# Low parts of the weights by transfers that add the raw tile onto the negated rounded one, in a two-block transformer kernel

## The chip, the cores and the metric

The kernel runs on one core of a Trainium2 chip. The metric is the device time of one execution in microseconds (us), the median of several runs. Engines are named TensorE (PE in the profile, PEld for its weight loads), VectorE (DVE), ScalarE (ACT), GpSimd (POOL) and SyncE (SP); 16 DMA engines move data for all of them.

## The reference, cut to what matters

The program is a chain of dense layers on 512 tokens of width 1024, all in fp32: a mixer with pooling and a gated spatial branch, a feed-forward layer with a convolution, a gated embedding layer, then two layers of feed-forward, attention, feed-forward. Nearly all arithmetic is activations times a weight matrix that is read once:

```python
def swiglu(h, wg, wu, wd):
    return (jax.nn.silu(h @ wg) * (h @ wu)) @ wd
...
for i in range(DEPTH_2):
    x = x + 0.5 * swiglu(rmsnorm_2(x, ffn_norm1[i]), ffn1_wg[i], ffn1_wu[i], ffn1_wd[i])
    h = rmsnorm_2(x, mix_norm[i])
    ...
    x = x + 0.5 * swiglu(rmsnorm_2(x, ffn_norm2[i]), ffn2_wg[i], ffn2_wu[i], ffn2_wd[i])
```

with inner widths of 2816 in the feed-forward layers and 1024 to 5120 elsewhere.

## The kernel before, in words

**Split products.** TensorE multiplies in a rounded format (fp32r in the profile). To keep fp32 accuracy each operand is split into a rounded part h and a low part lo = raw - h, and a product is three matmuls: h·h, h·lo and lo·h. A weight tile is 128x1024 (CH = 1024 columns, 512 KB) in nearly all places; it holds 8 blocks of 128x128, so 24 matmuls use it. `Weights._load` brings a raw tile (`wr`) from memory by a transfer on SyncE's queue (L717 to L720), `_split` takes two more tiles, `wh` and `wl`, and calls `_parts` (L728): ScalarE copies raw into `wh`, which rounds it, and VectorE writes raw - `wh` into `wl`. The first weight tile is handled in four pieces of 256 columns (`first`), and some tiles of the attention stages are 512, 416 or 384 columns wide. `wr`, `wh`, `wl`, `ws` and the activations' operand tiles (`op`, `opf`, `th`, `tl`, `tt`, `bb`) all share one pool of 34 buffers.

**Plain and fast stages.** The mixer, the convolution layer, the embedding layer, the first feed-forward layer and the attentions use each weight tile as it is. The other three feed-forward layers (`fast_swiglu`) save one product in eight by Strassen's scheme: `_sums` (L733) loads 4 raw tiles, makes 3 sums and differences on VectorE (`ws`, and one raw tile that is overwritten), and splits 7 tiles in all; each is used by 24 matmuls with 256 columns. This is a block; a stage has 9 of them. `fast_order` sets the order: 8 plain tiles first (4 pairs), then blocks, with the tiles of the down projection ("down chunks") in between, 16 before the end of the last block and 6 after it.

**The order of the work.** The program is first recorded as a list of operations. `Order.arrange` (a list scheduler with its own costs, buffer counts and transfer times) then decides in which order the operations stand on each engine; each engine executes its own list in order and waits on semaphores for what it needs. `Weights.next` records the load and split of a tile four tiles ahead of its use (AHEAD = 3), and the scheduler may move them further ahead as buffers allow. All operations are emitted at L691, so every row of the profile has that line and the tiles' names tell them apart. Transfers of weights stand on SyncE's queue, five small transfers (positions, bias table, p) on GpSimd's; GpSimd otherwise does some elementwise work in the mixer and the softmax products of the attentions.

Of the kernel before, what the change touches and what calls it, by code (L numbers as in the profile page):

```python
# [10 lines left out]
F32 = mybir.dt.float32  # L11
# [3 lines left out]
AF = mybir.ActivationFunctionType  # L15
ALU = mybir.AluOpType
# [13 lines left out]
CH = 1024  # L30
# [666 lines left out]
class Weights:  # L697
# [28 lines left out]
        return h, lo  # L726

    def _parts(self, raw, h, lo):  # L728
        self.nc.scalar.copy(out=h, in_=raw)
        self.nc.vector.tensor_tensor(out=lo, in0=raw, in1=h.bitcast(F32), op=ALU.subtract)  # L730


    def _sums(self):  # L733
# [1209 lines left out]
```

## Time and profile before

| | |
|---|---|
| median of 3 runs | 2630.89 us (2630.42 to 2632.65) |
| the profiled execution | 2632.25 us, of which the span is 2630.5 us |
| TensorE busy | 2605.5 us (99%) |
| VectorE busy | 1846.0 us (70%) |
| ScalarE busy | 1072.0 us (41%) |
| GpSimd busy | 126.3 us (5%) |
| DMA queue of SyncE | 251.31 MB, 28.9% of 16 engines' span |
| software queue (GpSimd) | 0.92 MB, 0.1% |

The span is the profiled execution from its first to its last instruction. A busy share is an average over stages with different limits; matmuls are pipelined, so the mean time of one matmul is longer than the step from one to the next. The granted TensorE clock is full (0.9 or more) in all slices of the page. TensorE is never idle for long, and the chain of work that ended last runs through its matmuls.

### The profile page before, as it was taken

The page shows a single profiled execution, that of the slowest core. Times are in us where ns is not written, and L with a number is a line of the kernel's source. Part 1 is how long each engine was busy: PE and PEld are TensorE (multiplying, and loading weights), DVE is VectorE, ACT ScalarE, POOL GpSimd, SP SyncE. Part 2 cuts the span into 40 slices and gives each one's busy share as a digit, 9 for nine tenths or more (in the row PEclk, how much of TensorE's full clock was granted, in tenths as well). Part 3 has the DMA queues.
Part 4 walks back from the last instruction along what each step waited for, and adds up shares of the span by engine and source line. Part 5 has one row for each costly group of instructions (what it writes and reads, how often), then busy time and mean ns, then how long its engine had stood idle before and what let it go on. Part 6 is the DMA issues. An engine that isn't in the chain of part 4 may idle for free. (4 is left out here: it accounts for less than half of the span.)

```text
span 2630.5 us, 36927 instructions
## 1 busy us (share of the span) xinstructions
PE 2605.5 (99%) x14732; PEld 2225.9 (85%) x14732; DVE 1846.0 (70%) x3076; ACT 1072.0 (41%) x1658; POOL 126.3 (5%) x193
## 2 busy tenths in 40 slices
PE   9999999999999999999999999999999999999999
PEld 7888888888888888889788999889999866789998
DVE  7525487969957944445778777787777686787774
ACT  5333333323444323233743433533434475543342
POOL 1100000000000000001400000000000142000000
PEclk9999999999999999999999999999999999999999
DMA  5232232333322423234131323413233101213332
GB/s 200 96 113 79 98 111 72 98 119 121 116 93 81 133 82 122 88 98 132 52 112 57 111 99 105 153 33 112 89 105 136 31 17 61 88 57 113 105 104 81
DMA packets 103037, 254.60 MB, mean 97 GB/s; under 512 B 37376, under 2 KB 39296, under 8 KB 102864
## 3 DMA queue, kind: packets, MB, share of 16 engines
q1 hardware_dynamic: 102560, 251.31, 28.9%
q8 instruction: 116, 1.90, 0.3%
q0 software_dynamic: 304, 0.92, 0.1%
q14 instruction: 57, 0.47, 0.1%
HBM read 242.76 MB, written 9.44 MB: 96 GB/s over the span
## 5 line engine op out<-in xcount | busy, mean ns | idle before, releaser
L691 PE MATMUL ps<-op,wh 128*128 128x512 f32 x3840 | 1194.9, 392 | 3.4 <-ACT wh L691 2.4
L691 PEld LDWEIGHTS ps<-op,wh 128*128 128x128 f32 x3840 | 717.6, 188 | 157.4 <-issue 5.2
L691 PE MATMUL ps<-op,wl 128*128 128x512 f32 x1920 | 749.5, 390 | 0.0
L691 DVE TENSOR_TENSOR wl<-wr,wh 128x1024 fp32r<-128x1024 f32 (+3 forms) x471 | 543.6, 1162 | 126.3 <-ACT wh L691 55.5
L691 ACT CAST wh<-wr 128x1024 fp32r<-128x1024 f32 (+3 forms) x471 | 459.9, 991 | 324.5 <-DMA wr<-in_w 170.8
L691 PEld LDWEIGHTS ps<-op,wl 128*128 128x128 f32 x1920 | 360.4, 188 | 76.3 <-issue 1.2
L691 DVE TENSOR_TENSOR f<-ps,f 128x512 f32<-128x512 f32 x233 | 160.1, 689 | 251.0 <-PE ps L691 209.6
L691 PE MATMUL pt<-op,wh 128*128 128x512 f32 x1056 | 326.3, 391 | 3.4 <-ACT op L691 3.3
L691 PE MATMUL ps<-th,wl 128*128 128x256 f32 x864 | 244.5, 283 | 0.0
L691 PE MATMUL ps<-tl,wh 128*128 128x256 f32 x864 | 244.5, 283 | 0.0
L691 PE MATMUL ps<-th,wh 128*128 128x256 f32 x864 | 244.4, 283 | 0.0
L691 PE MATMUL ps<-bb,wh 128*128 128x256 f32 x1296 | 236.8, 283 | 0.0
L691 PEld LDWEIGHTS pt<-op,wh 128*128 128x128 f32 x1056 | 196.3, 188 | 45.3 <-ACT op L691 4.5
L691 PE MATMUL pt<-op,wl 128*128 128x512 f32 x528 | 205.0, 389 | 0.0
L691 PEld LDWEIGHTS ps<-bb,wh 128*128 128x128 f32 x1296 | 202.2, 192 | 0.0
L691 PE MATMUL ps<-bb,wl 128*128 128x256 f32 x648 | 183.4, 283 | 0.0
L691 ACT CAST op<-f 128x512 fp32r<-128x512 f32 x136 | 83.2, 620 | 238.7 <-DVE f L691 218.9
L691 PEld LDWEIGHTS ps<-tl,wh 128*128 128x128 f32 x864 | 165.8, 192 | 1.0
L691 PEld LDWEIGHTS ps<-th,wh 128*128 128x128 f32 x864 | 165.8, 192 | 0.9
L691 PEld LDWEIGHTS ps<-th,wl 128*128 128x128 f32 x864 | 165.8, 192 | 0.1
L691 PE MATMUL ps<-wh,op 128*128 128x256 f32 (+3 forms) x608 | 147.9, 330 | 0.3 <-ACT opf L691 0.3
L691 DVE TENSOR_TENSOR f<-f 128x512 f32<-128x512 f32 (+1 forms) x186 | 121.0, 651 | 35.3 <-ACT f L691 25.8
(211 smaller groups left out, 2829.6 us busy)
## 6 DMA issues: line engine op xcount, KB each, us to landing
wr<-in_w SPq DMA_DIRECT2D x411, 512.0 KB, 4.2
wr<-in_w SPq DMA_DIRECT2D x40, 256.0 KB, 2.8
bias<-e SPq DMA_DIRECT2D x28, 256.0 KB, 2.9
opf<-bias SPq DMA_DIRECT2D x16, 448.0 KB, 4.2
x<-in_xT SPq DMA_DIRECT2D x8, 256.0 KB, 4.5
out_y<-x SPq DMA_DIRECT2D x7, 256.0 KB, 2.0
wr<-in_w SPq DMA_DIRECT2D x4, 416.0 KB, 6.1
wr<-in_w SPq DMA_DIRECT2D x12, 128.0 KB, 4.1
```

Source lines behind the costliest of these rows:

```text
L691: getattr(getattr(self.nc, o.eng), o.name)(*[real(a) for a in o.args], **{k: real(v) for k, v in o.kw.items()})
```

## The change

For tiles of 1024 columns the subtraction on VectorE is dropped. ScalarE, which has just written the rounded tile `wh`, writes its negative into `wl` by a second activation (scale -1), and a transfer from GpSimd's queue then adds the raw tile onto `wl` (`accum_op`). Narrower tiles keep the subtraction. The transfer reads `wr` (or `ws`) and `wl` from on-chip memory and writes `wl`; `wr` cannot be reused, and `wl` cannot be multiplied with, before it has landed.

```diff
     def _parts(self, raw, h, lo):
-        self.nc.scalar.copy(out=h, in_=raw)
-        self.nc.vector.tensor_tensor(out=lo, in0=raw, in1=h.bitcast(F32), op=ALU.subtract)
+        nc = self.nc
+        nc.scalar.copy(out=h, in_=raw)
+        if raw.shape[1] == CH:
+            nc.scalar.activation(out=lo, in_=h.bitcast(F32), func=AF.Copy, scale=-1.0)
+            nc.gpsimd.dma_start(out=lo, in_=raw, accum_op=ALU.add)
+        else:
+            nc.vector.tensor_tensor(out=lo, in0=raw, in1=h.bitcast(F32), op=ALU.subtract)
```

The scheduler sees other operations with other costs, so the order on all engines is made anew. 492 transfers of the form `wl<-wr` or `wl<-ws` now stand on GpSimd.

ScalarE at the first block of the first fast stage, before (CAST is the rounding copy, `ps` are TensorE's sums that ScalarE evicts):

```order
L691 CAST wh<-ws 128x1024 x2
L691 CAST op<-f 128x512
L691 CAST wh<-wr 128x1024 x2
L691 CAST wh<-ws 128x1024
L691 CAST wh<-wr 128x1024
L691 COPY f<-ps 128x512
L691 CAST wh<-wr 128x1024
L691 ACTIVATE f<-ps 128x256
```

The same place with the change:

```order
L691 CAST wh<-ws 128x1024
L691 ACTIVATE wl<-wh 128x1024 x2
L691 CAST wh<-wr 128x1024
L691 ACTIVATE wl<-wh 128x1024 x2
L691 CAST wh<-wr 128x1024
L691 ACTIVATE wl<-wh 128x1024 x2
L691 CAST wh<-ws 128x1024
L691 ACTIVATE wl<-wh 128x1024
L691 COPY f<-ps 128x512
```

Each rounding copy is followed by a negation, often of the tile before, and the eviction of `ps` stands behind them.

GpSimd between the last softmax product of the first attention and the second attention, before (no weight work at all):

```order
L691 TENSOR_TENSOR opf<-opf,aden 128x128
L691 TENSOR_TENSOR opf<-opf,aden 128x768
L691 COPY opf<-bkrot 128x4x32 x2
L691 TENSOR_TENSOR f<-opf,tcbqr 128x128
L691 TENSOR_TENSOR f<-opf,tsbqr 128x4x16
```

GpSimd at the first block of the first fast stage with the change, each transfer with the semaphores that it waits for (DMAHW: transfers of SyncE's queue, DMASW: of GpSimd's own, the rest are engines):

```order
L691 DMA wl<-ws 128x1024 [waits DMASW6_49,DVE_49,Activation_49]
L691 DMA wl<-wr 128x1024 [waits DMAHW3_49,DMASW1_49,Activation_49]
L691 DMA wl<-wr 128x1024 [waits DMASW2_49,DVE_49,Activation_49]
L691 DMA wl<-ws 128x1024 [waits DMASW7_49,DMASW5_49,Activation_49]
L691 DMA wl<-wr 128x1024 [waits DMASW3_49,DMAHW4_49,DMASW0_49,Activation_49]
L691 DMA wl<-wr 128x1024 [waits DMAHW2_49,DMASW6_49,Activation_49]
L691 DMA wl<-ws 128x1024 [waits DMASW4_49,DVE_49,Activation_49]
```

The seven tiles of a block are seven transfers in a row, each behind ScalarE's negation.

TensorE at the start of the program, at the second weight tile, before (`mcol` matmuls are the mean of squares):

```order
L691 MATMUL ps<-op,wh 128x512 [waits Activation_49]
L691 MATMUL ps<-op,wl 128x512 [waits DVE_49]
L691 MATMUL ps<-op,wh 128x512 x2
L691 MATMUL ps<-op,wl 128x512
L691 MATMUL ps<-op,wh 128x512 x2
```

The same place with the change:

```order
L691 MATMUL ps<-op,wh 128x512 [waits Activation_49]
L691 MATMUL ps<-op,wh 128x512
L691 MATMUL pt<-mcol,f 128x1 [waits DVE_49]
L691 MATMUL pt<-mcol,f 128x1 x3
L691 MATMUL ps<-op,wh 128x512 [waits Activation_49]
L691 MATMUL ps<-op,wh 128x512
L691 MATMUL ps<-op,wh 128x512 [waits PE_49,Activation_49]
L691 MATMUL ps<-op,wh 128x512
L691 MATMUL pt<-f,ones 128x512 [waits DVE_49]
L691 MATMUL ps<-op,wl 128x512 [waits DMASW0_49]
```

TensorE now does the matmuls with rounded weights and the two norm matmuls first, and comes to its first transferred low part behind them.

## Rows read from the trace of the kernel before

**Rows 1.** Section 1 of the page: busy us (share) xinstructions:

```profile
PE 2605.5 (99%) x14732; PEld 2225.9 (85%) x14732; DVE 1846.0 (70%) x3076; ACT 1072.0 (41%) x1658; POOL 126.3 (5%) x193
```

**Rows 2.** TensorE's waits: what it waited for: total us, times, longest:

```profile
PE pt L691 <- ACT op L691: 3.3, 3, 1.1
...
PE pt L691 <- DVE opf L691: 2.7, 1, 2.7
...
PE ps L691 <- DVE op L691: 1.4, 3, 0.7
PE pt L691 <- DVE op L691: 1.2, 1, 1.2
```

**Rows 3.** Chain that ended last, in order of time: start us, us, what:

```profile
2418.40 20.15 PE ps L691 x168
2438.55 10.91 PE pt L691 x48
...
2573.70 20.15 PE ps L691 x168
2593.85 32.68 PE pt L691 x144
```

**Rows 4.** VectorE groups, 2418.4 to 2449.46: xcount | busy us, mean ns | idle:

```profile
L691 DVE TENSOR_TENSOR wl<-wr,wh 128x1024 fp32r<-128x1024 f32 x6 | 7.3, 1221 | 0.3
L691 DVE TENSOR_TENSOR wl<-ws,wh 128x1024 fp32r<-128x1024 f32 x3 | 3.7, 1223 | 1.2 <-ACT wh L691 1.2
```

**Rows 5.** DMA, 2418.4 to 2449.46: packets, MB, share; issues, us to landing:

```profile
q1 hardware_dynamic: 864, 3.15, 30.7%
...
wr<-in_w SPq DMA_DIRECT2D x6, 512.0 KB, 3.6
```

**Rows 6.** Stretches: length; busy of PE, PEld, DVE, ACT, POOL; clock; DMA share:

```profile
900.00:1000.00 100.00, 100.00 (x463) 82.72 (x462) 51.42 (x112) 24.44 (x30) 0.00 (x0) 1.00 0.31 95
2418.40:2449.46 31.06, 31.06 (x218) 29.17 (x218) 22.70 (x27) 11.82 (x15) 0.00 (x0) 1.00 0.31 103
```

**Rows 7.** VectorE on low parts, 900 to 1000 us: count, min/median/max ns:

```profile
L691 DVE TENSOR_TENSOR wl<-wr,wh x17: 1215/1218/1227, 900.3 to 994.7; 128x1024 fp32r<-128x1024 f32 x17
```

**Rows 8.** Groups by shape, whole span: xcount | busy us, mean ns:

```profile
L691 DVE TENSOR_TENSOR wl<-wr,wh 128x1024 fp32r<-128x1024 f32 x411 | 500.4, 1226 | 123.4 <-ACT wh L691 55.1 <-PE ps L691 50.9 <-PE pt L691 7.6
L691 ACT CAST wh<-wr 128x1024 fp32r<-128x1024 f32 x411 | 425.6, 1046 | 316.4 <-DMA wr<-in_w 167.9 <-PE ps L691 74.0 <-DVE wl L691 37.9
...
L691 DVE TENSOR_TENSOR wl<-ws,wh 128x1024 fp32r<-128x1024 f32 x81 | 98.9, 1221 | 11.0 <-ACT wh L691 10.4
```

**Rows 9.** GpSimd at L691: count, min/median/max ns, first and last start:

```profile
L691 POOL DMA_DIRECT2D f<-in_pT x2: 536/536/536, 680.5 to 681.7; - x2
```

**Rows 10.** DMA issues, whole span: xcount, KB each, us to landing:

```profile
f<-in_pT POOLq DMA_DIRECT2D x2, 256.0 KB, 2.8
```

**Rows 11.** VectorE on low parts, 2320 to 2630.5: ns, first and last start:

```profile
L691 DVE TENSOR_TENSOR wl<-ws,wh x27: 1215/1219/1226, 2328.0 to 2577.5; 128x1024 fp32r<-128x1024 f32 x27
```

**Rows 12.** DMA, 2.5 to 30 us: packets; queue; issues, us to landing:

```profile
DMA packets 4342, 10.44 MB, mean 380 GB/s; under 512 B 482, under 2 KB 1001, under 8 KB 4341
...
q1 hardware_dynamic: 4341, 10.42, 100.0%
...
wr<-in_w SPq DMA_DIRECT2D x12, 512.0 KB, 7.2
```

**Rows 13.** ScalarE in order of time, 12 to 26 us: start us, us, operation:

```profile
14.51 1.98 ACT L691 CAST wh<-wr 128x1024 fp32r<-128x1024 f32 x2
```

**Rows 14.** TensorE in order of time, 14 to 24 us: start us, us, operation:

```profile
17.06 0.50 PE L691 MATMUL ps<-op,wl 128*128 128x512 f32 x1
```

## The prediction

> **What bounds the kernel now.** I read the page first. TensorE is busy 2605.5 of 2630.5 us [rows 1], so all its idle time is 25 us, and the list of what it waits for has no entry above 3.3 us [rows 2]; low parts that come late are not in it. Waits on VectorE results are a handful of us. So lighter VectorE work can give back almost nothing: TensorE's own stream is the time, and the question is only whether the new way delivers low parts as fast as TensorE eats them.
>
> For that I looked for the place where it eats fastest. The chain of waits shows it [rows 3]: in the three fast feed-forward stages a block of 168 matmuls lasts 20.15 us and is followed by down chunks, 48 matmuls in 10.91 us. A weight tile takes part in 24 matmuls, so a block uses 168 / 24 = 7 split tiles, one each 2.88 us, and a down chunk lasts 10.91 / 2 = 5.45 us, the pace of a plain stage too. In one block with two down chunks (2418.40 to 2449.46, 31.06 us) VectorE makes 6 + 3 = 9 low parts [rows 4], and the DMA engines bring 6 raw tiles at 30.7% of their time [rows 5]. A plain stretch of 100 us has 17 low parts and a DMA share of 0.31 [rows 6, 7].
>
> **What the change removes.** 411 + 81 = 492 subtractions of 1.22 us, some 600 us of VectorE [rows 8], none of it on the path: VectorE is at 22.70 of 31.06 us in the block stretch [rows 6] and TensorE stands at 31.06 of 31.06. Worth: under the 25 us of idle time, and by the waits on VectorE in [rows 2] (2.7 + 1.4 + 1.2 us and smaller) some 5 us. I book nothing.
>
> **What it adds on ScalarE.** 492 activations on 128x1024; the nearest row is the cast of the same shape, 1046 ns [rows 8], so 515 us. In the block stretch that is 9 x 1.05 = 9.4 on top of 11.82 us [rows 6]: 21 of 31 us. Casts and evictions queue behind an activation for 1 us at most. Cost nothing, while the low parts keep a few us of cover (below).
>
> **What it adds on GpSimd.** 492 transfer issues. A transfer of 128 rows from this queue held GpSimd for 536 ns [rows 9]; nine are 4.8 us of 31. An adding transfer may take longer to describe; it would have to take over 3.4 us to bind (rivals). GpSimd's queue is in order: the wait of one transfer for its activation holds the next ones and, in the attention stages, the softmax products; there few weights are split.
>
> **Latency.** Before, a low part is there 1.2 us after the rounded tile. Now it is activation 1.05 + issue 0.54 + landing. The nearest landings are 2.8 us for 256 KB from the GpSimd queue [rows 10] and 3.6 us for 512 KB loads [rows 5], so 4.4 to 5.2 us in all with free DMA engines, 3 to 4 us later than now. Cover: in the last block the last sum's subtraction starts at 2577.5 [rows 11] and ends 1.2 us later, while its product, the seventh, starts 2.88 us before 2593.85 [rows 3], at 2591.0: 12 us ahead. So latency alone is hidden in steady state. Raw tiles are also held longer, until the transfer has landed, and the subtractions that overwrite a sum (ws, in place) wait for it on VectorE with the evictions behind them; 4 us of 12 again. If the cover were gone, each late tile would cost its lateness.
>
> **Throughput, the term that decides.** Each adding transfer must read the raw tile, read the negated tile and write the sum, 512 KB each. No row shows such a transfer, so I bound it by loads of 512 KB. Kept full, the engines moved 380 GB/s at a share of 100% [rows 12]: 524288 B / 380 GB/s = 1.38 us per tile. In the block stretch a load took 30.7% of 31.06 us / 6 = 1.59 us [rows 5]. If the two reads go side by side and the write is hidden, an addition costs one load, 1.38 us; if the reads share what one read has now, two loads, 2.76 to 3.18 us; if nothing overlaps, three, from 4.14 us. I take two loads: a transfer's pace today is that of one stream in and one out, and an addition has two in. Between the two prices I take the middle, 2.97 us, and 1.485 us for a load.
>
> One fast stage, from the first block to the end of the last, is 9 blocks and 16 down chunks: TensorE 9 x 20.15 + 16 x 5.45 = 268.6 us. The DMA engines have 9 x 7 + 16 = 79 additions and 9 x 4 + 16 = 52 loads (a block loads 4 tiles, the other 3 of its 7 are sums). At 2.97: 79 x 2.97 + 52 x 1.485 = 234.6 + 77.2 = 311.8 us. That is 43.2 us over TensorE's time, so TensorE waits, and three such stages give **+130 us**. At 2.76 and 1.38 it is 289.8, +21 each, +64; at 3.18 and 1.59 it is 333.9, +65 each, +196. At one load it is 180.8, hidden. The point from which it decides is (268.6 - 77.2) / 79 = 2.42 us. The chunks behind the last block and the eight plain ones ahead of the first have slack, but what TensorE lost in the blocks does not come back there.
>
> A plain stretch needs 17 x 2.97 + 31 = 81 of 100 us: covered, nothing booked.
>
> The Trainium skill, "Collectives: The Full Stack", section "The bandwidth ceiling: the fold count and why AG ≠ RS ≠ AR", says that an adding transfer is slower than a copy not through its arithmetic but because it has two sources to read through one ring, with 1.93 as the measured ratio. No run here shows that yet; by it an addition would cost an estimated 1.93 x 1.485 = 2.87 us and the three stages +105 us.
>
> **Start.** From 2.5 to 30 us the engines are at 100% [rows 12]. The first full tile is rounded by ScalarE from 14.51 us in a pair of casts and TensorE uses its low part at 17.06 [rows 13, 14]. Now: casts to 16.5, activation to 17.5, issue to 18.1, then a landing like that of the loads there, 7.2 us [rows 12]: 25.3 us. The new order (ahead) puts the rounded-only matmuls of four blocks and two norm matmuls first: eight steps of 10.91 / 48 = 0.23 us [rows 3] behind the casts, which carries TensorE from 16.5 to some 19 us. So some 6 us (0 to 12) are lost once. The later tiles follow in steps of a chunk.
>
> **Sum.** The profiled execution took 2632.25 us with a span of 2630.5; the median of the runs is 2630.89. 2631 + 130 + 6 = **2767 us**; with the two prices 2631 + 64 to 2631 + 196 + 12, that is 2695 to 2839.
>
> **Rivals.**
> 1. *Not slower.* The additions cost less than 2.42 us, since the reads run side by side (the price of one load, 1.38). Place: the same blocks; then the DMA engines need 181 to 268 us against 268.6, TensorE never waits, and the time is 2631 less up to some 5 us of VectorE waits, plus 0 to 6 at the start: 2626 to 2637. For it: DMA shares of 0.31 leave much room. Against: at 380 GB/s and 100% a plain copy is already at what the engines give, and an addition moves half as much again.
> 2. *Three passes.* The read of the destination, the read of the raw tile and the write follow each other: 4.14 us at least. One stage: 79 x 4.14 + 52 x 1.38 = 398.9, +130; three: +391. The other 492 - 237 = 255 tiles need 4.14 + 1.38 = 5.52 against 5.45 us: +18. 2631 + 391 + 18 + 6 = 3046 us, and more at the dearer price. For it: nothing in this trace shows the engines reading a tile that they also write. Against: no row either; it is only the dearest way to do it.
> 3. *GpSimd is the bound.* An issue takes over 268.6 / 79 = 3.4 us, six times the 536 ns, in which TensorE waits for GpSimd with idle DMA engines. At 3.5 us: 276.5 against 268.6, +8 per stage, 2631 + 24 + 6 = 2661. Against: six times is a lot for a third operand.
>
> That the change does only part of what it says is out: the order shows 492 transfers on GpSimd; the narrower tiles stay on VectorE.
>
> **Chances and range.** Forecast (two loads, 2695 to 2839, with tails where queues mesh badly) 0.50; rival 1 0.14 (0.10 of it within 0.2%, 0.04 faster); rival 2 0.25, half of it above 3080; rival 3 0.11. What a measurement of this kernel can tell from no change is about 0.2%, or 5 us. Faster 0.04, same 0.10, slower 0.86. The range runs from 2628, the middle of rival 1, to 3080, which takes in rival 2 at its cheapest; some 0.18 is left out.
>
> **What will show it.** Right: TensorE's largest wait is that of low-part matmuls for transfers into wl; its idle time lies in the stretches with blocks, at 10 to 20% of them, and the plain stretches stay full; a block with two down chunks grows from 31.06 to some 36 us; the DMA share in it is 0.9 or more; the software queue's share of the span is near 492 x 2.97 / 2630 = 55%; VectorE falls to some 1250 us, ScalarE rises to some 1590. Wrong by rival 1: DMA share in blocks 0.6 to 0.8 and no such waits. By rival 2: software queue's share beyond 75%, waits in plain stages too. By rival 3: GpSimd near 100% in blocks, DMA engines idle beside it. I would also be wrong if the additions disturb the loads, so that TensorE waits for rounded tiles: then the first waits are ScalarE's on raw tiles.

## The result, and the profile after

The changed kernel takes 2943.55 us (median; 2934.70 to 2951.62), the kernel before 2631.77 us on the same chip: a ratio of 1.1183, 95% interval 1.1148 to 1.1218, or +312 us. The forecast was 2767 us, +136: slower as it said, inside its range, but less than half of the loss. The profiled execution has a span of 2949.8 us.

All rows of the kernel after are from it. First its page: busy times (beside [rows 1]), the DMA queues (q0 is GpSimd's, q1 SyncE's; packets, MB, share of 16 engines) and the issues with their time to landing (beside [rows 5, 10]).

```profile
PE 2707.1 (92%) x14732; PEld 2293.1 (78%) x14732; DVE 1292.4 (44%) x2584; ACT 1546.1 (52%) x2150; POOL 544.2 (18%) x685
...
q0 software_dynamic: 71152, 258.90, 46.9%
q1 hardware_dynamic: 102560, 251.31, 25.1%
...
wr<-in_w SPq DMA_DIRECT2D x411, 512.0 KB, 5.9
wl<-wr POOLq DMA_DIRECT2D x411, 512.0 KB, 6.4
wl<-ws POOLq DMA_DIRECT2D x81, 512.0 KB, 7.4
```

TensorE's idle time went from 25 to 2949.8 - 2707.1 = 242.7 us, +218; its busy time rose by 102 us although the matmuls are the same. One addition took 46.9% x 2949.8 / 492 = 2.81 us of all 16 engines, near the 2.97 of the forecast. But it lands in 6.4 to 7.4 us, and raw tiles in 5.9 (before, over the whole span, in 4.2).

TensorE's longest waits after, beside [rows 2], where none was above 3.3 us (total us, times, longest):

```profile
PE ps L691 <- DMA wl<-wr: 68.7, 39, 4.7
PE ps L691 <- DVE f L691: 38.8, 20, 6.1
PE pt L691 <- DMA wl<-wr: 25.6, 13, 5.0
PE pt L691 <- DVE f L691: 21.9, 7, 4.9
PE ps L691 <- ACT op L691: 20.3, 4, 15.0
PE ps L691 <- DMA wl<-ws: 17.2, 16, 3.4
```

Late low parts are first with 68.7 + 25.6 + 17.2 = 111.5 us, but the waits on VectorE and ScalarE, which are at 44% and 52%, add up to as much with smaller rows. Why they are late is in the groups of GpSimd and ScalarE (xcount | busy, mean ns | idle before, its main releaser), and in ScalarE's and VectorE's waits:

```profile
L691 POOL DMA_DIRECT2D wl<-wr x411 | 354.8, 865 | 1764.0 <-ACT wl L691 1526.6
L691 ACT ACTIVATE wl<-wh 128x1024 fp32r<-128x1024 f32 x492 | 517.3, 1057 | 306.5 <-DMA wl<-wr 198.0
L691 ACT CAST wh<-wr 128x1024 fp32r<-128x1024 f32 (+3 forms) x471 | 460.8, 985 | 389.3 <-DMA wr<-in_w 174.8
```

```profile
DVE f L691 <- ACT f L691: 526.4, 169, 14.3
...
ACT wl L691 <- DMA wl<-wr: 198.0, 72, 6.5
...
ACT wh L691 <- DMA wr<-in_w: 174.8, 46, 11.3
ACT wh L691 <- DMA wl<-wr: 140.0, 52, 8.3
```

The same two waits before:

```profile
DVE f L691 <- ACT f L691: 94.7, 93, 3.2
```

```profile
ACT wh L691 <- DMA wr<-in_w: 170.8, 85, 5.4
```

ScalarE's waits for raw tiles are in sum what they were, 174.8 us for 170.8, though single ones are longer. New are its waits for adding transfers, which hold buffers of the pool until they land: all of its waits for transfers into `wl` add up to 497 us, where it waited 49 us for VectorE's low parts before. What stands behind the stopped casts and negations in ScalarE's list, evictions and operand casts, stops with them. One such place can be followed in order of time, first on ScalarE and VectorE, then on TensorE (start us, us, operation, in brackets the idle time before it and what ended it):

```profile
746.86 1.04 ACT L691 CAST wh<-wr 128x1024 fp32r<-128x1024 f32 x1 [4.13 <-DMA wl<-wr]
747.81 0.81 ACT L691 ACTIVATE f<-f,vec 128x512 f32<-128x512 f32 x1
748.52 1.99 ACT L691 ACTIVATE wl<-wh 128x1024 fp32r<-128x1024 f32 x2
750.42 1.98 ACT L691 CAST wh<-wr 128x1024 fp32r<-128x1024 f32 x2
752.30 0.61 ACT L691 CAST op<-f 128x512 fp32r<-128x512 f32 x1
```

```profile
748.65 0.75 DVE L691 SCALAR_TENSOR_TENSOR f<-f,vec 128x512 f32<-128x512 f32 x1 [6.61 <-ACT f L691]
```

```profile
752.96 1.56 PE L691 MATMUL ps<-op,wh 128*128 128x512 f32 x2 [15.02 <-ACT op L691]
```

A cast waits 4.13 us for a landing; the activation behind it is what VectorE waits 6.61 us for; VectorE's result goes back to ScalarE's cast into `op` at 752.30, which ends 15 us without a matmul. Of this wait, which the profile puts down to "ACT op", 4.13 us are thus a wait for a transfer, and some 4 us more are the negations and casts of weights at 748.52 and 750.42, which stand in the list ahead of the cast that TensorE needs.

**Where the 312 us are.** The three fast stages, from the first block to the end of the last, before and then after (length, busy of PE, PEld, DVE, ACT, POOL; granted clock; DMA share; GB/s):

```profile
1415.98:1676.96 260.98, 260.90 (x1862) 246.95 (x1861) 199.90 (x230) 106.71 (x130) 0.00 (x0) 1.00 0.32 108
1764.50:2025.47 260.97, 260.89 (x1862) 246.94 (x1861) 199.71 (x230) 106.42 (x130) 0.00 (x0) 1.00 0.32 108
2335.96:2593.85 257.89, 257.89 (x1850) 244.63 (x1849) 197.48 (x226) 106.36 (x130) 0.00 (x0) 1.00 0.31 105
```

```profile
1484.92:1821.23 336.31, 283.99 (x1850) 262.25 (x1849) 107.61 (x146) 177.17 (x203) 65.77 (x77) 0.93 0.86 198
1921.57:2265.09 343.52, 285.36 (x1850) 263.02 (x1849) 109.14 (x149) 177.34 (x204) 66.14 (x77) 0.93 0.85 195
2574.78:2911.87 337.09, 282.79 (x1850) 260.88 (x1849) 107.88 (x146) 176.74 (x204) 65.42 (x76) 0.94 0.85 197
```

They lose 75.3 + 82.6 + 79.2 = 237 us; TensorE's busy time in them rises by 72 us, its idle time by 165. The first block starts at 1484.92 in place of 1415.98: another 69. The rest, some 13, lies between the stages. Within a stage the loss sits in the blocks. Two blocks of the last stage and the chunks between two blocks, after:

```profile
2716.44:2743.71 27.27, 21.58 (x170) 20.56 (x169) 6.24 (x8) 13.68 (x16) 5.59 (x7) 1.00 0.99 235
...
2838.69:2869.11 30.42, 24.07 (x170) 23.45 (x169) 6.09 (x10) 12.75 (x14) 5.17 (x6) 0.89 0.82 195
```

```profile
2743.71:2755.20 11.49, 11.04 (x50) 8.78 (x48) 6.53 (x9) 6.52 (x8) 1.72 (x2) 1.00 0.59 137
```

and the same place before, a block and the two chunks behind it:

```profile
2449.30:2469.61 20.31, 20.31 (x170) 20.31 (x169) 15.05 (x16) 8.43 (x10) 0.00 (x0) 1.00 0.37 130
```

```profile
2469.61:2480.36 10.75, 10.75 (x50) 8.86 (x49) 9.52 (x12) 4.61 (x6) 0.00 (x0) 1.00 0.15 49
```

The nine blocks of this stage grew from 182.84 to 248.46 us, the chunks between them from 75.05 to 88.63. In blocks the DMA engines are at 0.82 to 1.00, between them at 0.51 to 0.79: full where they are needed, with room beside it that isn't used.

### The profile page after: what moved, and what is told of

Same layout as the page of the kernel before. It is cut to its first block, busy times and chain, and to the rows that moved or that the text cites. A ratio compares the mean times of both kernels' runs of the same rounds, so it can differ in the third digit from the quotient of the medians.

```text
span 2949.8 us, 38558 instructions
## 1 busy us (share of the span) xinstructions
PE 2707.1 (92%) x14732; PEld 2293.1 (78%) x14732; DVE 1292.4 (44%) x2584; ACT 1546.1 (52%) x2150; POOL 544.2 (18%) x685
## 3 DMA queue, kind: packets, MB, share of 16 engines
q0 software_dynamic: 71152, 258.90, 46.9%
q1 hardware_dynamic: 102560, 251.31, 25.1%
## 5 line engine op out<-in xcount | busy, mean ns | idle before, releaser
L691 PE MATMUL ps<-op,wh 128*128 128x512 f32 x3840 | 1206.2, 395 | 22.3 <-ACT op L691 19.9
L691 PEld LDWEIGHTS ps<-op,wh 128*128 128x128 f32 x3840 | 725.0, 190 | 181.6 <-ACT op L691 21.2
L691 PE MATMUL ps<-op,wl 128*128 128x512 f32 x1920 | 754.8, 393 | 0.0
L691 POOL DMA_DIRECT2D wl<-wr x411 | 354.8, 865 | 1764.0 <-ACT wl L691 1526.6
L691 ACT ACTIVATE wl<-wh 128x1024 fp32r<-128x1024 f32 x492 | 517.3, 1057 | 306.5 <-DMA wl<-wr 198.0
L691 ACT CAST wh<-wr 128x1024 fp32r<-128x1024 f32 (+3 forms) x471 | 460.8, 985 | 389.3 <-DMA wr<-in_w 174.8
L691 PEld LDWEIGHTS ps<-op,wl 128*128 128x128 f32 x1920 | 363.8, 190 | 76.7 <-issue 1.4
L691 DVE TENSOR_TENSOR f<-ps,f 128x512 f32<-128x512 f32 x233 | 159.8, 689 | 498.9 <-PE ps L691 255.2
L691 PE MATMUL pt<-op,wh 128*128 128x512 f32 x1056 | 333.6, 397 | 5.8 <-DVE op L691 3.3
L691 PE MATMUL ps<-th,wl 128*128 128x256 f32 x864 | 268.3, 311 | 68.1 <-DMA wl<-wr 56.0
L691 PE MATMUL ps<-th,wh 128*128 128x256 f32 x864 | 266.6, 309 | 54.9 <-DVE f L691 38.8
L691 PE MATMUL ps<-tl,wh 128*128 128x256 f32 x864 | 262.6, 304 | 0.0
L691 PEld LDWEIGHTS ps<-th,wl 128*128 128x128 f32 x864 | 185.3, 214 | 76.0 <-DMA wl<-wr 61.7
L691 PE MATMUL ps<-bb,wh 128*128 128x256 f32 x1296 | 240.0, 285 | 0.0
L691 PEld LDWEIGHTS pt<-op,wh 128*128 128x128 f32 x1056 | 200.6, 192 | 49.4 <-DVE op L691 4.6
L691 PE MATMUL pt<-op,wl 128*128 128x512 f32 x528 | 211.2, 400 | 25.8 <-DMA wl<-wr 25.6
L691 PEld LDWEIGHTS ps<-th,wh 128*128 128x128 f32 x864 | 185.1, 214 | 62.0 <-DVE f L691 43.4
L691 PEld LDWEIGHTS ps<-bb,wh 128*128 128x128 f32 x1296 | 204.7, 194 | 0.0
L691 PE MATMUL ps<-bb,wl 128*128 128x256 f32 x648 | 186.8, 288 | 18.1 <-DMA wl<-wr 12.7
L691 PEld LDWEIGHTS ps<-tl,wh 128*128 128x128 f32 x864 | 185.1, 214 | 0.9
L691 DVE TENSOR_TENSOR f<-f 128x512 f32<-128x512 f32 (+1 forms) x186 | 121.3, 653 | 130.0 <-ACT f L691 114.0
L691 ACT CAST op<-f 128x512 fp32r<-128x512 f32 x136 | 81.8, 617 | 152.8 <-DVE f L691 120.8
```

The lines of the kernel that those rows point to most:

```text
L691: getattr(getattr(self.nc, o.eng), o.name)(*[real(a) for a in o.args], **{k: real(v) for k, v in o.kw.items()})
```

## The experiments

All but those that say otherwise were made from the changed kernel; the loss is the median less that of the kernel before on the same chip, and intervals are those of the ratio. Two readings compete throughout: the **load** (the engines' time is the bound) and the **lateness** (a low part comes later than the lists were ordered for, holds its buffers, and the lists stop).

### The parts of the change

**VectorE adds in place of the transfer.**

```diff
-            nc.gpsimd.dma_start(out=lo, in_=raw, accum_op=ALU.add)
+            nc.vector.tensor_tensor(out=lo, in0=raw, in1=lo.bitcast(F32), op=ALU.add)
```

> The changed kernel, but the raw tile is added onto the negated one by VectorE (1.22 us) in place of the transfer; ScalarE's 492 negations stay. Theory T (the engines' time for the additions, 2.81 us each, is the bound) and theory S (buffers and in-order queues wait for landings of 6.4 to 7.4 us) both expect the time of before: 2626 to 2645 us. Rival A (ScalarE's added 517 us and the new order are what costs) expects over 2700 us.

Measured: 2632.35 us, ratio 1.0004 (0.9995 to 1.0014). The negation on ScalarE and a newly made order cost nothing; the transfer, with what hangs on it, is the whole loss.

**A plain copy.**

```diff
-            nc.gpsimd.dma_start(out=lo, in_=raw, accum_op=ALU.add)
+            nc.gpsimd.dma_start(out=lo, in_=raw)
```

> The changed kernel with the transfers as plain copies of the raw tile into wl, without the addition (the low parts are then the raw weights; the amount of work on all other engines is unchanged). T: one read per tile, 1.4 to 1.5 us; a fast stage needs 79 x 1.45 + 78 = 193 us of the engines against TensorE's 261, so 2635 to 2660 us. S: a copy still has to be issued and to land, some 4 to 5 us, so a good part of the loss stays: 2700 to 2800 us.

Measured: 2679.55 us, 1.0186 (1.0171 to 1.0201), +49, between what the two readings had; the order of every engine is that of the change. Its queue and issues:

```profile
q0 software_dynamic: 71152, 258.90, 27.3%
...
wl<-wr POOLq DMA_DIRECT2D x411, 512.0 KB, 3.7
wl<-ws POOLq DMA_DIRECT2D x81, 512.0 KB, 4.2
```

A copy takes 27.3% x 2682.3 / 492 = 1.49 us of the engines and holds GpSimd for 0.53 us; the sum makes it 2.81 and 0.865. So 263 of the 312 us come with the addition.

**The negation on GpSimd.**

```diff
-            nc.scalar.activation(out=lo, in_=h.bitcast(F32), func=AF.Copy, scale=-1.0)
+            nc.gpsimd.tensor_scalar(out=lo, in0=h.bitcast(F32), scalar1=-1.0, scalar2=None, op0=ALU.mult)
```

> The changed kernel with the negation on GpSimd in place of ScalarE, so that waits for a free buffer hold GpSimd's list alone and no eviction or rounding queues behind them. T: no change, 2910 to 2970 us. S, in the form that ScalarE's list is blocked: 2760 to 2850 us. If GpSimd's negation takes over 2.2 us, nine of them and nine issues fill a block with two down chunks (31 us), and it is slower than 2970 us.

Measured: 3246.18 us, 1.2342 (1.2321 to 1.2363). GpSimd needs 3.12 us for a negation and 1.20 for an issue, so the seven tiles of a block take it 30 us of work, where TensorE needs 20. It is busy for 61% of this span, and for 18% in the change.

### Size and place

**Half of the columns added** (the other half is left as the negated tile; the planner is made to count twice the bytes of an addition, so that the order of the engines stays that of the change), and **half added, half subtracted on VectorE**.

```diff
-            o.bytes = 4 * math.prod(v.shape)
+            o.bytes = 4 * math.prod(v.shape) * (2 if "accum_op" in kw else 1)
...
-            nc.gpsimd.dma_start(out=lo, in_=raw, accum_op=ALU.add)
+            nc.gpsimd.dma_start(out=lo[:, :CH // 2], in_=raw[:, :CH // 2], accum_op=ALU.add)
```

> The order of all engines is that of the changed kernel, row for row; ScalarE negates the whole tile, but the transfer adds only the left 512 columns (the right half of each low part is left as the negated rounded weight). So each addition has half the bytes, 1.4 to 1.5 us of the engines and a landing of some 4 us, as the plain copies had. T and S both expect the time of the plain copies, 2665 to 2700 us: what a transfer takes counts, not that it adds. If the adding itself is dear in another way (issue, order of landings): over 2750 us.

```diff
-            nc.scalar.activation(out=lo, in_=h.bitcast(F32), func=AF.Copy, scale=-1.0)
-            nc.gpsimd.dma_start(out=lo, in_=raw, accum_op=ALU.add)
+            c, d = slice(0, CH // 2), slice(CH // 2, CH)
+            nc.scalar.activation(out=lo[:, c], in_=h[:, c].bitcast(F32), func=AF.Copy, scale=-1.0)
+            nc.gpsimd.dma_start(out=lo[:, c], in_=raw[:, c], accum_op=ALU.add)
+            nc.vector.tensor_tensor(out=lo[:, d], in0=raw[:, d], in1=h[:, d].bitcast(F32), op=ALU.subtract)
```

> Only the left 512 columns of each tile go by negation and adding transfer, the right 512 by VectorE's subtraction. As many transfers and waits as in the changed kernel, each of half the bytes. T: 1.4 us each, 79 x 1.4 + 78 = 189 us of the engines per fast stage against 261: 2635 to 2660 us. S: landings of some 4 to 5 us still hold buffers and queues: 2700 to 2800 us.

Measured: 2765.72 us, 1.0511 (1.0495 to 1.0526), +134; and 2790.08 us, 1.0608 (1.0585 to 1.0630), +159, where VectorE's list stops too (297 us on rounded tiles, 142 on transfers that hold buffers). The half addition takes the engines 27.1% x 2765.4 / 492 = 1.52 us, as much as the plain copy of a whole tile, and yet loses 85 us more. One of its blocks:

```profile
2587.56:2617.73 30.17, 23.72 (x170) 23.31 (x169) 5.93 (x9) 14.42 (x16) 6.02 (x7) 0.89 0.62 149
```

It is as slow as a block of the change with the engines at 0.62. Load alone is not the cause. With the same order and the same time of the engines, what differs from the copy in the rows is 0.865 us of issue for 0.53, and 4.1 us of landing for 3.7; whether an addition hinders in some further way was not tried.

**Additions in blocks only**, VectorE elsewhere, and the reverse (the sum's split passes `sums=True`).

```diff
...
-        if raw.shape[1] == CH:
+        if raw.shape[1] == CH and sums:
...
```

> Adding transfers only for the 189 tiles of the Strassen blocks; all other tiles keep VectorE's subtraction. T: a fast stage has 63 x 2.81 + 52 x 1.5 = 255 us for the engines against TensorE's 261, so 2631 to 2665 us. S: in a block every tile still waits as now, and a stage loses most of its 79 us: 2780 to 2850 us.

> The reverse: adding transfers for the 303 tiles outside the blocks, subtractions in the blocks. Both theories: a fast stage is back at 261 us with 16 additions. The start (6 us) and the 69 us that the changed kernel loses ahead of the first block stay: 2640 to 2710 us. If the losses of this run and of the one with blocks only sum to clearly less than 312 us, the two kinds of tiles hinder each other.

Measured: 2793.04 us, 1.0621 (1.0600 to 1.0643), +162, stages of 310 to 313 us; and 2731.51 us, 1.0385 (1.0365 to 1.0405), +100, more than either reading had (2640 to 2710), first block at 1481.14, stages of 275, 270 and 258 us. So the 65 to 69 us ahead of the blocks come from tiles outside them. Together 262 of 312: the two disturb each other a little.

### The planner and the buffers

**The planner told**: it counts twice the bytes and a landing of 4.5 us for additions, 8.0 us in all, where the change has 3.6.

```diff
-            o.bytes = 4 * math.prod(v.shape)
+            o.bytes = 4 * math.prod(v.shape) * (2 if "accum_op" in kw else 1)
...
-                    end = dma + 1500.0
+                    end = dma + (4500.0 if "accum_op" in o.kw else 1500.0)
```

> The changed kernel, but the scheduler that makes the order is told that an addition takes twice the bytes and lands 4.5 us behind its data in place of 1.5. T: the engines are the bound whatever the order, 2900 to 2960 us. S in the form of a bad order (ScalarE and VectorE come to a blocked row too early): 2720 to 2850 us. S in the form of too few buffers: small gain, 2870 to 2930 us.

Measured: 2888.53 us, 1.0977 (1.0960 to 1.0994), +257. An order made for the true landing gets back 55 us of 312.

**30 buffers in place of 34**, with the change and in the kernel before.

```diff
-        self.opp = pool("op", 34)
+        self.opp = pool("op", 30)
```

> The change with 30 in place of 34 buffers in the pool from which raw, rounded and low parts come, and all else by the same planner. Theory 'late low parts hold buffers, and ScalarE's list stops on them': 60 to 150 us above the 2943.5 of the change, 3000 to 3100. Theory 'the engines' time is the bound': their work is the same, 2930 to 2960.

> The kernel before (VectorE subtracts) with 30 in place of 34 buffers, the control of the run above. A low part is there 1.2 us after its rounded tile, so buffers come free early: both theories expect 2631 to 2660 us.

Measured: 3124.36 us with the change, 181 above it and more than either reading had; 2722.47 us for the kernel before, 1.0345 (1.0327 to 1.0362), +91. The control missed what was expected of it: the kernel before has no buffers to spare over its whole span either. In the fast stages, where it loses little, the two stand apart. The middle stage with 30 buffers, before and with the change:

```profile
1811.18:2080.20 269.02, 266.41 (x1870) 250.45 (x1871) 205.12 (x232) 106.36 (x131) 0.00 (x0) 0.99 0.33 102
```

```profile
1996.62:2387.61 390.99, 306.73 (x1871) 278.21 (x1870) 113.31 (x151) 181.63 (x206) 66.30 (x77) 0.90 0.75 169
```

Against 34 buffers that is +8 us for the kernel before and +47 for the change, and the change got slower while the engines' share fell from 0.85 to 0.75: fewer buffers, not more load.

### Load against lateness

**A copy, and a second transfer that nobody waits for** (a resident table to a scratch).

```diff
-            nc.gpsimd.dma_start(out=lo, in_=raw, accum_op=ALU.add)
+            a = nc.gpsimd.dma_start(out=lo, in_=raw)
+            b = nc.gpsimd.dma_start(out=self.dram.tile([P, 2, CH // 2], F32, name="jd", tag="jd", bufs=64),
+                                    in_=self.con[:, :CH // 2].unsqueeze(1).to_broadcast([P, 2, CH // 2]))
+            b.deps.add(a)
+            b.bytes = 0
...
```

> As the plain copy (the low part is left as the raw weight, and the activation's result is overwritten), and GpSimd issues behind each of the 492 copies a second transfer of 512 KB, from a resident table to a scratch in DRAM, for which nobody waits. So the DMA engines get about the 2 x 1.49 = 2.98 us per tile that an addition takes (2.81), but what a low part waits for is only its copy. Theory 'the engines' time is the bound': as slow as the change or slower, 2920 to 3000 us. Theory 'the time from a tile's cast to its low part is what costs': the landing of the copies tells it; if that stays at 4 to 4.5 us, beside 3.7 to 4.2 of the plain copy alone, 2690 to 2780 us, and only if the second transfers push it to 6 us or more does the time come near that of the change.

Measured: 2817.48 us, 1.0707 (1.0689 to 1.0724), +186, with 49.9% of the span on that queue, more than the change's 46.9%. Landings of the copies are 5.6 to 5.7 us, and each second transfer holds GpSimd for another 0.77 us. Like load as in the change with a shorter landing costs 126 us less than it, but 137 more than the copy: neither reading alone.

**The copy as two halves.**

```diff
-            nc.gpsimd.dma_start(out=lo, in_=raw, accum_op=ALU.add)
+            for c in (slice(0, CH // 2), slice(CH // 2, CH)):
+                nc.gpsimd.dma_start(out=lo[:, c], in_=raw[:, c])
```

> As the plain copy (the low part is left as the raw weight), but each copy is issued as two of 512 columns, so that GpSimd holds a tile for 2 x 0.53 = 1.06 us in place of 0.53, and the bytes and the engines' time stay. The addition of one half only had an issue of 0.87 us and a landing of 4.1 and lost 134 us, the plain copy with 0.53 and 3.7 lost 49. Theory 'every part of the time from cast to low part costs, the issue too': 2730 to 2800 us. Rival 'an issue costs nothing of itself, an adding transfer disturbs in another way': 2675 to 2700 us, as the plain copy.

Measured: 2725.66 us, 1.0359 (1.0343 to 1.0374), +94: 46 us more than the copy for 0.53 us more of issue, with the queue at 30.9% in place of 27.3%. The rival (as the plain copy) fell; the reading that the issue counts had a little more.

**VectorE adds, and a copy of 8 columns follows** that the products wait for; and **the same with the planner told** (2.2 us counted, known as a whole tile).

```diff
-            nc.gpsimd.dma_start(out=lo, in_=raw, accum_op=ALU.add)
+            a = nc.vector.tensor_tensor(out=lo, in0=raw, in1=lo.bitcast(F32), op=ALU.add)
+            b = nc.gpsimd.dma_start(out=lo[:, :8], in_=raw[:, :8])
+            b.bytes = 0
```

With the planner told, `b.bytes = 0` is left out, and the planner takes the copy for one of the whole tile when it looks for what waits for it:

```diff
+                if name == "dma_start" and v.base.name == "wl":
+                    box = [(0, n) for n in v.base.shape]
```

> As the addition on VectorE (2632.4 us, no loss), and behind each of the 492 additions GpSimd issues a copy of 8 columns (4 KB) of the raw tile onto the low part, which the products and the buffers wait for; the planner counts nothing for it (the low part's first 8 columns are left as the raw weight). The DMA engines get almost nothing to do, and the low part comes later by an issue of 0.53 us and the landing of a small transfer, some 2 to 2.8 us: 2.5 to 3.3 us in all. Theory 'lateness is what costs, whatever the engines do': 2645 to 2700 us (the plain copy, 1.05 + 0.53 + 3.7 us in place of 1.2, so 4.1 us later, lost 49). Theory 'the engines' load costs': 2631 to 2640.

> As the addition on VectorE with a small copy behind it (first 8 columns left as the raw weight), which lost 102 us with 0.53 us of issue and 1.7 of landing; but here the planner that orders the lists counts 2.2 us for it and knows that every product waits for it, where it counted some 0.2 before. The real lateness is the same. Theory 'lateness against the order costs: each engine's list stops on a result that the list's order has due earlier': 2631 to 2660 us. Theory 'lateness costs by itself, by the buffers that it holds': 2700 to 2740.

Measured: 2733.10 us, 1.0392 (1.0374 to 1.0409), +102, with the queue at 3.7% and landings of 1.7 us, more than lateness was given (2645 to 2700); told, 2650.49 us, 1.0069 (1.0054 to 1.0084), +18. The middle stage, untold and told:

```profile
1806.38:2094.10 287.72, 267.29 (x1862) 250.37 (x1861) 199.25 (x228) 180.05 (x206) 41.17 (x78) 0.99 0.36 101
```

```profile
1777.52:2039.28 261.76, 259.13 (x1850) 244.89 (x1849) 196.14 (x226) 180.82 (x206) 40.55 (x77) 1.00 0.39 110
```

This is the cleanest pair: the same transfers with the same 0.53 + 1.7 us, and DMA engines hardly busier than before, lose 102 us in an order made without them and 18 in one made with them. A lateness of 2 us costs by the order it meets.

**VectorE adds, and two full transfers follow that nobody waits for**, from a resident table; and **the same from the tile's own low part**, so that they can't run ahead (the edit shown).

```diff
-            nc.gpsimd.dma_start(out=lo, in_=raw, accum_op=ALU.add)
+            nc.vector.tensor_tensor(out=lo, in0=raw, in1=lo.bitcast(F32), op=ALU.add)
+            for _ in range(2):
+                b = nc.gpsimd.dma_start(out=self.dram.tile([P, CH], F32, name="jd", tag="jd", bufs=64),
+                                        in_=lo.bitcast(F32))
+                b.bytes = 0
...
```

> As the addition on VectorE (no loss), and behind each addition GpSimd issues two transfers of 512 KB from a resident table to a scratch in DRAM, for which nobody waits: the engines get per tile some 2.9 us as in the change, and no low part waits for a transfer. Theory 'lateness is what costs': what is late here is the loads alone, whose landing goes from 3.6 to some 6 us; they are issued a buffer's life ahead, so 2635 to 2680 us. Theory 'the engines' load costs': as the copy with a second transfer or the change, 2820 to 2950.

> As the addition on VectorE and the two transfers nobody waits for, but these now read the tile's own low part (2 x 512 KB to a scratch in DRAM), so that they can't be issued before it is made and come one tile at a time. In the run with a resident source they ran ahead in bursts: some slices of the span had the engines at 99%, others at 20%. Theory 'the engines' load costs, through late loads of raw tiles': 2800 to 2920 us, ScalarE's casts waiting for raw tiles. Theory 'lateness of the low parts against the time for which the lists were ordered is what costs': 2635 to 2690 us, the loads being issued well ahead.

Measured: 2910.67 us, 1.1059 (1.1042 to 1.1075), +279, in bursts; paced, 2775.27 us, 1.0550 (1.0533 to 1.0568), +143. The first shows a stretch with the extra transfers and full engines and, further on, one without them:

```profile
2000.00:2034.00 34.00, 22.63 (x163) 21.93 (x164) 20.06 (x22) 19.67 (x21) 12.77 (x20) 0.85 1.00 375
2180.00:2256.87 76.87, 76.87 (x554) 72.87 (x554) 57.58 (x66) 54.67 (x64) 0.00 (x0) 1.00 0.39 128
```

The paced one carries per tile 47.3% x 2774.9 / 984 x 2 = 2.67 us of load, near the change's 2.81, with no low part late, though its transfers hold the low parts' buffers (ScalarE waits 35 us for that, SyncE's queue 62). Its raw tiles land in 7.0 us, and ScalarE's casts wait 250 us for them, against 136.5 with the vector addition alone:

```profile
ACT wh L691 <- DMA wr<-in_w: 250.4, 84, 6.8
```

So such a load costs 143 us when paced and 279 in bursts, as the waits show in the main through the raw tiles: the reading that only lateness of low parts counts is refuted. But a full share of the engines doesn't stop TensorE by itself, as this block of the last stage of the paced run shows:

```profile
2713.57:2733.88 20.31, 20.31 (x170) 20.31 (x169) 12.64 (x14) 15.41 (x18) 7.95 (x15) 1.00 0.96 361
```

Both kinds of extra transfer write to DRAM, where an addition writes to on-chip memory; whether that matters was not tried.

**The copy with the planner told** (4.8 us counted in place of 3.6).

```diff
-                    end = dma + 1500.0
+                    end = dma + (2700.0 if o.eng == "gpsimd" else 1500.0)
```

> As the plain copy (low part left as the raw weight), which lost 49 us with 0.53 us of issue and 3.7 to 4.2 of landing, where the planner counts 3.6 in all; here it counts 4.8. Theory 'lateness against the order': 2631 to 2655 us. Theory 'buffers held': 2675 to 2700, as the plain copy. With the change itself a planner told of 8 us still lost 257 us, so there the buffers bind under either.

Measured: 2699.59 us, 1.0250 (1.0233 to 1.0267), +68, 20 us worse than untold. Telling helped the small transfer and the additions, not the copy; raw tiles land in 5.0 us here, which no planner was told, and each low part is given more room among 34 buffers. Which of the two it is was not tried.

### What they say together

For a transfer the planner counts 0.06 us of issue, 0.6 and 1.5 us around it and its bytes at 368 GB/s, 3.6 us for 512 KB; nothing for the untold small copy but 0.2 us between engines.

| kernel | issue + landing, us | counted by the planner, us | loss, us |
|---|---|---|---|
| small copy, told | 0.53 + 1.7 | 2.2 | 18 |
| plain copy | 0.53 + 3.7 | 3.6 | 49 |
| plain copy, told | 0.53 + 3.9 | 4.8 | 68 |
| copy in halves | 1.06 + 3.4 | 3.6 | 94 |
| small copy, untold | 0.53 + 1.7 | 0.2 | 102 |
| half addition | 0.87 + 4.1 | 3.6 | 134 |
| copy and load | 0.55 + 5.7 | 3.6 | 186 |
| the change | 0.87 + 6.4 | 3.6 | 312 |
| the change, told | 0.87 + 6.4 | 8.0 | 257 |

For the plain copy, the copy in halves and the half addition the engines' time per tile is alike (1.49, 1.71 and 1.52 us), and the loss rises with the excess over what the planner counted (0.6, 0.9 and 1.4 us). With more load too it goes on rising (2.7 us for copy and load, 3.7 for the change). The excess isn't all: the untold small copy has 2.0 us with hardly any load and loses less than the half addition, and the change and the copy that are told lose 257 and 68 us with no excess left. ScalarE's waits for transfers into `wl` go with the loss, 185, 250, 288 and 497 us for the copy, the halves, the half addition and the change. Shown are a loss by load without late low parts (143, a part of it by held buffers), a loss by lateness without load (102, 84 of it given back by another order), and that buffers bind (181 us for four of them). The 312 us hold all three at once; how they share it is not settled, since the change has more load and more lateness than either.

## Why the prediction was right and wrong, step by step

- **The subtractions are worth nothing; the negation costs nothing.** Right: the vector addition with all else changed is at 1.0004.
- **Issue on GpSimd.** 0.54 us was taken from a plain transfer [rows 9]; an adding one holds GpSimd for 0.865. This is far from the 3.4 us of rival 3, which fell, but the 0.33 us are part of each low part's way.
- **The price of an addition.** Right: 2.81 us against 2.97, two loads' worth. Rival 1 (under 2.42) and rival 2 (over 4.14) fell on it. Against the plain copy on the same queue it is 2.81 / 1.49 = 1.89. The Trainium skill, "Collectives: The Full Stack", section "The bandwidth ceiling: the fold count and why AG ≠ RS ≠ AR", gives 1.93 as the measured ratio for a collective whose add needs two source reads; the 1.89 here agrees, and no run here shows what makes it.
- **"Latency alone is hidden", by 12 us of cover.** This step failed: it booked nothing, and the plain copy, whose load is hidden by the prediction's own sum, lost 49 us. The landing was taken from lightly loaded engines (2.8 to 3.6 us, [rows 5, 10], with a share of 0.31 in [rows 5]) and is 6.4 to 7.4 us in the change. And the cover was read at one tile, the last sum of the last block, and taken for slack. It is the room that the lists were ordered for: 2.2 us of unplanned lateness lose 102 us, some 27 of them in the middle fast stage. Four buffers less lose 91 us in the kernel before, though 8 in that stage. The waits for buffers had been seen ("raw tiles are also held longer"), and were put into the same 12 us.
- **The stage sum: engines full for 311.8 us.** The place was right for most of the loss, the averaging failed. The sum spread 79 additions over blocks and chunks alike (with 16 chunks in a stage; between its blocks the trace has 14). By the measured prices (2.81, and 25.1% x 2949.8 / 479 tiles = 1.54 for a load) it would be 79 x 2.81 + 52 x 1.54 = 302 us, while a block alone needs 7 x 2.81 + 4 x 1.54 = 25.8 us against 20.3. With the chunks not helping, that is 9 x 5.5 = 50 us a stage, 149 us in three; the blocks of the last stage last 20.9 to 30.4 us with the engines at 0.82 to 1.00. The mean in [rows 6] had hidden this already: its DMA share of 0.31 is a mean over a block at 0.47 and two chunks at 0.01. The 149 us are an estimate. That leaves 237 - 149 = 88 us of the stages without a sum: the chunks grew too, with engines that are not full, and 72 us of the 237 are slower matmuls (below).
- **Plain stretches cost nothing.** Right where they are steady: from 900 to 1200 us TensorE is busy for 300.00 of 300.00 us at a share of 0.81. Wrong elsewhere. The stretches ahead of the first block, after:

```profile
0.00:200.00 200.00, 179.44 (x758) 144.98 (x759) 60.07 (x137) 105.45 (x128) 46.32 (x54) 0.95 0.86 219
200.00:700.00 500.00, 495.67 (x2561) 407.82 (x2560) 253.85 (x479) 250.40 (x305) 70.07 (x83) 0.99 0.75 179
700.00:900.00 200.00, 178.56 (x826) 144.82 (x825) 105.25 (x201) 107.84 (x146) 26.97 (x32) 0.93 0.71 175
900.00:1200.00 300.00, 300.00 (x1465) 247.51 (x1464) 103.02 (x225) 140.83 (x161) 47.87 (x57) 1.00 0.81 194
1200.00:1485.00 285.00, 274.70 (x1594) 235.02 (x1593) 161.71 (x442) 156.63 (x326) 60.82 (x67) 0.98 0.51 133
```

  In the first 200 us TensorE is idle for 20.6 us (5.3 before). The start itself is the smaller part; its first 30 us, before and after:

```profile
0.00:30.00 30.00, 24.70 (x103) 18.16 (x104) 24.02 (x43) 20.48 (x31) 5.91 (x6) 1.00 0.95 355
```

```profile
0.00:30.00 30.00, 19.70 (x63) 13.29 (x64) 16.69 (x44) 24.31 (x35) 8.12 (x12) 0.84 0.95 317
```

  That is 10.3 us idle for 5.3, 5 us more where 6 were forecast: this term was right, but for the lower clock. Another 10.3 us are one wait for ScalarE between 100 and 200 us. The convolution's stretch, 700 to 900 us, has 21.4 us (0.1 before): there ScalarE's list carries both the weights and what TensorE needs next, as in the rows at 746.86.
- **TensorE's own time was taken as fixed.** It isn't. Behind the 15 us of idle time at 752.96 the granted clock is 0.50, which is 1.2 GHz, for some 4 us with 9 matmuls; then it is 1.00 (2.4 GHz), with 20 matmuls in as long:

```profile
752.96:757.00 4.04, 4.04 (x9) 2.88 (x10) 4.04 (x8) 2.74 (x4) 1.71 (x2) 0.50 1.05 197
758.00:762.00 4.00, 4.00 (x20) 3.29 (x19) 0.71 (x2) 2.78 (x3) 1.71 (x2) 1.00 1.05 198
```

  In 20 of the 27 blocks of the fast stages the mean granted clock is 0.84 to 0.94, where it was 1.00 in all before. Matmuls that take longer are 102 us of the loss (the group on `th,wl` has a mean of 311 ns, before 283). A microsecond of additional idle time came with 102 / 218 = 0.47 us of that.
- **"I would also be wrong if the additions disturb the loads."** Loads do land later (5.9 us for 4.2), but the sign that was named did not come: TensorE's largest wait is for low parts, its waits for rounded tiles are 1.3 us, and ScalarE's waits for raw tiles are 175 us, where they were 171 before.

The step that failed is thus the latency that was booked at nothing, with the buffers that it holds; beside it, the sum over a whole stage and a clock taken as fixed. The forecast's 130 us for the stages are near the 36 + 34 + 37 = 107 us that the three stages lose under the paced load, but that nearness proves little: that run's blocks can be full and lose nothing. The prediction's range held the result only by the chance that it gave to the dearer rival.

## What to carry to other kernels

Before work is moved to a longer way, ask not how far ahead of its use a result now lies, but for what time the order and the buffers were made: in a kernel at 99% of one engine, room that looks like slack may be the plan itself. Taking a few buffers away from the kernel before tests this cheaply, if the result is read stage by stage. Make the sum of a shared resource over the shortest stretch that must balance by itself (here a block), not over a stage. And take a landing from a stretch as loaded as the one to come: the transfers that were there before get later too.

## What the runs showed of the hardware

- A transfer that adds onto its destination took 2.81 us of the 16 engines per 512 KB, the copy on the same queue 1.49; its issue held GpSimd for 0.865 us at 512 KB and at 256 KB alike (1.20 where GpSimd also made the negations), a copy's for 0.53.
- A copy of 4 KB in 128 rows landed in 1.7 us, of 512 KB in 3.7, an addition of 256 KB in 4.1 and of 512 KB in 6.4 to 7.4 under the change's load.
- GpSimd's negation of a 128x1024 tile took 3.12 us; ScalarE's took 1.06.
